# The turn from attention to the MLP: last residual rows in temporary tiles, later stores, block pieces at other steps, one weight load issued earlier

## The chip, the core and the metric

The kernel runs on one core of a Trainium2 chip. A core has TensorE (matrix products, into PSUM), VectorE (DVE), ScalarE (ACT), GpSimd (POOL) and SyncE (SP), each working through its own instructions in order. SyncE's queue issues nearly all transfers between the chip's memory and the core's SBUF; 16 DMA engines carry them out. The metric is the device time of one execution in microseconds (us); lower is better.

## The reference

One layer of an encoder over x of 2048 tokens x 1024 features, all in float32:

```python
sh1, sc1, gt1, sh2, sc2, gt2 = split(silu(c) @ w_ada + b_ada, 6)
h = rmsnorm(x, g_norm1) * (1 + sc1) + sh1
q_sb, k_sb, v_sb, q_ca, k_ca, v_ca = split(h @ w_in)
o_sb = stick_breaking_attention(q_sb, k_sb, v_sb)      # 8 heads of 64, strictly causal
o_ca = chunked_relpos_attention(rmsnorm(q_ca, g_q), rmsnorm(k_ca, g_k), v_ca, rel_bias)
                                                       # 8 heads, own chunk of 64 + 8 before
x = x + gt1 * (concat(o_sb, o_ca) @ w_o)               # the output projection
h = rmsnorm(x, g_norm2) * (1 + sc2) + sh2
x = x + gt2 * (square(relu(h @ w1)) @ w2)              # the MLP, 1024 -> 4096 -> 1024
```

## The kernel before

Everything is held transposed: 128 features in the partitions, tokens along the free axis, in four token blocks `g` of 512 (`TB`), handled in the order 3, 2, 1, 0. A tile of 128 x 512 float32 is 256 KB. To keep float32 accuracy each operand is split into a high part (`act.copy` into float32r) and a low part (DVE: source minus high), and each product is three matmuls (`mm3`: high x high, high x low, low x high).

**Attention with filler.** After the input projections the attention units run in a loop of steps. Into its steps are woven single matmuls of a "filler": first input projections still missing, then the output projection `outproj(g)` of finished token blocks. A filler is a generator: it yields 1.0 after each matmul, and at the end of a row a function that finishes the row. One row `n` of `outproj` is 128 output features: 8 x 3 matmuls of the weights `ow` (1 MB, from `scr_wo`, ring of three buffers) with the attention output `fx`. At the start of row `n` the weights of row `n + 2` and the residual input `xr` of row `n + 1` are loaded. `finish_row` calls `residual`: DVE adds the gated row to `xr`, and the store of `xr` to `scr_x` is appended to the list `stores`.

**The turn.** When the attention loop ends, rows 3 to 7 of block 1 and all of block 0's output projection are left. `drain.append(True)` marks it, attention's pools are closed, and the MLP's pools are opened over the same memory (`temp`: 7 tiles, `kept`: 12 tiles, `opp`: 8 operand tiles). Then a hand-written list runs. `row()` finishes the matmuls of the current row and its residual, sends stores down to one left over, and starts the next row (its loads, its first matmul). Between the rows stand `steps[0].fetch(a, b)`, which loads operand tiles `opm` a to b - 1 of block 0's output projection (0.5 MB each from `scr_m`), and `some(k, m)`, piece `m` of operand block `k`.

**Operand blocks.** The MLP works on two halves of the tokens, first blocks 3 and 2 (`mb` = 1), with a seven-product scheme (Strassen's) for each 2 x 2 arrangement of tiles. `right_blocks(1, k)` for k = 0 to 3 makes the seven right operands `h` (`hops[i, k]`) of product `i` out of four stored rows. Its pieces are: 0, `load`: four loads of 256 KB from `scr_x` (`ty` for block 0, `cy` for the others); 1, `scale`: four multiplications on DVE, four affine steps and three high parts on ACT; 2, `mixed`: five DVE operations, two high parts on ACT; 3, `rest`: six DVE operations, two high parts on ACT.

**The Mixed and First steps.** After the last row a list `steps` runs, one entry at a time. The first eight are `Mixed` (the output projection of block 0, rows 5, 6, 7, 0, 1, 2, 3, 4; rows 5 to 7 find their weights still in the ring). Mixed step `n` is 24 matmuls (`pso`) over `opm` 0 to 7 and then a residual (`cxr`); `then()` loads the weights `wo` of the step three on, and from step 5 the first weights of the MLP (`w`, two loads of 512 KB), and has POOL form four sums of them (`ts`). Then come `First` steps, 12 matmuls each (4 blocks `k` x 3), in the order of products 1, 6, 5, 7, 2, 3, 4. Work can be tied to a step with `at(n, job)`: it is placed ahead of the step's matmuls. The left operands of the first two First steps, `opr`, are split at a place written by hand:

```python
            if n == KT - 2:
                firsts = spare.tile([P, 2, 2, TB], F32R, tag="r8", name="opr")
                for m in range(2):
                    steps[KT + m].prepare(firsts[:, m])
```

**Order on the queues.** In the turn SyncE keeps program order too (`osp`). Each transfer signals one of eight completion semaphores, taken in turn over all transfers of SyncE and ScalarE; a transfer is issued only when the eighth before it has landed, and when the tile it writes is free. A matmul on TensorE, DVE's and ACT's operations keep the order of the program.

Of the kernel before, what the change touches and what calls it, by code (L numbers as in the profile page):

```python
# [9 lines left out]
F32 = mybir.dt.float32  # L10
# [8 lines left out]
P = 128  # L19
# [5 lines left out]
KT = D // P  # L25
TB = 512
# [53 lines left out]
def encoder_kernel(ctx, tc, xT, c, g1, g2, w_in, w_rest, gqk, bias, w_o, w1, w2, w_ada, b_ada, out):  # L80
# [142 lines left out]
        )  # L223


    stores = []

    def residual(g, n, ps, xr):
        dve.scalar_tensor_tensor(xr, ps, mod[:, 2 * KT + n : 2 * KT + n + 1], xr, op0=ALU.mult, op1=ALU.add)
        stores.append(lambda: sp.dma_start(scr_x[g, n], xr))  # L230

    def load_residual(g, n, pl):
        xr = pl.tile([P, TB], F32, tag="xr", name=f"xr{g}_{n}")
        sp.dma_start(xr, xT[n * P : (n + 1) * P, g * TB : (g + 1) * TB])
        return xr

# [6 lines left out]
    if True:  # L243
# [260 lines left out]
        first = (2, 0, 1)  # L504
# [151 lines left out]
    if True:  # L656
# [317 lines left out]
        def outproj(self, g):  # L974
            yield lambda k: scr_m[g, k]

            def load(n):
                w = ring.tile([P, 2, KT, P], F32R, tag="r8", name=f"ow{g}_{n}")
                sp.dma_start(w.bitcast(F32), scr_wo[n,])
                return w  # L980

            mx = self.moving()
            ws = [load(0), load(1)]
            rx = load_residual(g, 0, xrp)
            yield "wait"
            for n in range(KT):
                w, xr = ws.pop(0), rx
                if g == 1:
                    resident[n] = w
                if n + 2 < KT:  # L990
                    ws.append(load(n + 2))
                if n + 1 < KT:
                    rx = load_residual(g, n + 1, xrp)
                else:
                    yield "ahead"
                ps = dense.tile([P, TB], F32, tag="ps", name=f"po{g}_{n}")
                for k in range(KT):
                    for i, (l, m) in enumerate(((0, 0), (0, 1), (1, 0))):
                        pe.matmul(
                            ps, w[:, l, k, :], mx[k][:, m, :], start=k == 0 and i == 0, stop=k == KT - 1 and i == 2  # L1000
                        )
                        yield 1.0
                yield lambda n=n, ps=ps, xr=xr: finish_row(g, n, ps, xr)
# [46 lines left out]
        weight = STEPS * sum(u.weight for u in units) + LAG * 0.6  # L1050
        credit = 0.0
        rest = 0
        late, soon, first, drain = [], [], [], []

        def fill(part):

# [20 lines left out]
        def force(f):  # L1077

            got = next(f.gen, None)
            if callable(got):  # L1080
                got()
            return None if got is None else callable(got)
# [87 lines left out]
    if True:  # L1170
# [25 lines left out]
        def temp(nm):  # L1196
            return tp.tile([P, TB], F32, tag="t", name=f"t{nm}")
# [9 lines left out]
        def at(n, job):  # L1207
            jobs.setdefault(n, []).append(job)
# [343 lines left out]
        for mb in (1, 0):  # L1552
            begin = len(steps)
            steps += [First(mb, j, i) for j in range(NP) for i in PRODUCTS]
            for j in range(NP):
                f = steps[begin + 7 * j]
# [22 lines left out]
        def some(k, *ns):  # L1579
            for n in ns:  # L1580
                blocks[k][n]()
# [3 lines left out]
        def row():  # L1585

            while force(left) is False:
                pass
            while len(stores) > 1:
                stores.pop(0)()  # L1590
            return force(left)

        steps[0].fetch(0, KT // 2)
        row()
        steps[0].fetch(KT // 2, KT - 2)
        some(0, 0)
        row()
        some(0, 1)
        steps[0].fetch(KT - 2, KT)
        row()  # L1600
        some(0, 2)
        some(1, 0)
        row()
        some(0, 3)
        some(1, 1)
        while row() is not None:
            pass
        while stores:
# [4 lines left out]
            del resident[n]  # L1613
        for m in range(LEFT):
            steps[m].load()
        at(0, lambda: some(2, 0))
        at(3, lambda: some(3, 0))
        for n, (k, m) in enumerate(((1, 2), (1, 3), (2, 1), (2, 2), (2, 3), (3, 1), (3, 2), (3, 3))):
            at(n, lambda k=k, m=m: some(k, m))
        ready, used = KT, 0  # L1620
        ahead = iter(steps[1:])
        nxt = next(ahead)
        for n, s in enumerate(steps):
            while nxt is not None and ready - used + nxt.tiles <= 8:
                nxt.prepare()
                ready += nxt.tiles
                nxt = next(ahead, None)
            for m in (0, 1) if n == 0 else (n + 1,):
                if m < KT:
                    steps[m].load_row()  # L1630
            if n == KT - 2:
                firsts = spare.tile([P, 2, 2, TB], F32R, tag="r8", name="opr")
                for m in range(2):
                    steps[KT + m].prepare(firsts[:, m])
            for job in jobs.get(n, ()):
                job()
            s.run()
            used += s.frees
            later.tick()
# [41 lines left out]
```

## Time and profile before

| | |
|---|---|
| median of 3 runs | 2691.01 us |
| lowest and highest | 2685.60 and 2695.53 us |
| the profiled execution | 2683.0 us |
| its span, first to last instruction | 2681.1 us |
| mean granted TensorE clock | 0.992 |
| TensorE busy | 2600.1 us, 97% |
| HBM read and written | 457.21 and 191.37 MB, 242 GB/s over the span |

The span is the time from the first to the last instruction of the profiled execution; the run's own time is 1.9 us longer. All times inside the trace count from the start of the span. "Busy" counts an engine's instructions, not its waiting; an idle stretch carries in brackets what ended it. "SPq" and "ACTq" are instructions that issue transfers. A program line of L42 is a helper that records the operation, so the tile names tell which part of the kernel a row belongs to.

### The profile page before, as it was taken

The numbers are of one execution on the slowest core, as the hardware profiler recorded it, in microseconds if no ns is written. First come the engines' busy times: TensorE is split into PE (matmuls) and PEld (weight loads), VectorE is DVE, ScalarE is ACT, GpSimd is POOL, SyncE is SP. The second block draws the span as 40 slices with busy tenths as digits, with TensorE's granted clock in tenths as the row PEclk, the third lists the DMA queues.
The fourth block names the chain that finished last, engine by engine and source line by source line (L and its number), as shares of the span: only waits on it lengthen the run. The fifth ranks groups of instructions, "written<-read, shape, count | busy, mean of one in ns | idle before, by whom it ended". The sixth has DMA issues, their size and how long they took to land. (4 is left out here: it accounts for less than half of the span.)

```text
span 2681.1 us, 40293 instructions
## 1 busy us (share of the span) xinstructions
PE 2600.1 (97%) x12944; PEld 2162.3 (81%) x12944; DVE 1919.8 (72%) x3287; ACT 1510.9 (56%) x2962; POOL 921.3 (34%) x1192
## 2 busy tenths in 40 slices
PE   7999999898999999999999999999999999999999
PEld 5888887687878887788877888878888888888887
DVE  7656766697789878889756777767857566655565
ACT  5333436786788778778644444456544445444443
POOL 4330145575566656777512233200002323200000
PEclk9999999999999999999999999999999999999999
DMA  9879888978887687756666777686675343465574
GB/s 340 306 300 364 308 322 256 265 255 275 252 255 247 203 269 246 232 190 211 211 231 248 278 256 273 252 334 219 217 265 188 138 165 138 149 243 194 198 267 157
DMA packets 263061, 651.28 MB, mean 243 GB/s; under 512 B 29632, under 2 KB 61376, under 8 KB 252992
## 3 DMA queue, kind: packets, MB, share of 16 engines
q1 hardware_dynamic: 261552, 643.98, 70.4%
q10 hardware_dynamic: 1296, 4.72, 0.4%
q8 instruction: 103, 1.69, 0.3%
q14 instruction: 110, 0.90, 0.1%
HBM read 457.21 MB, written 191.37 MB: 242 GB/s over the span
## 5 line engine op out<-in xcount | busy, mean ns | idle before, releaser
L42 PE MATMUL ps<-oph,opv 128*128 128x512 f32 x2688 | 612.0, 389 | 0.2
L42 PE MATMUL ps<-h,opw 128*128 128x512 f32 x2664 | 608.6, 391 | 1.9 <-DVE cx L42 1.9
L42 PEld LDWEIGHTS ps<-oph,opv 128*128 128x128 f32 x2688 | 504.0, 188 | 106.3 <-DVE opv L42 1.2
L42 PEld LDWEIGHTS ps<-h,opw 128*128 128x128 f32 x2664 | 502.6, 189 | 107.8 <-DVE cx L42 2.6
L42 POOL TENSOR_TENSOR b<-b,p 128x512 f32<-128x512 f32 (+1 forms) x320 | 359.6, 1124 | 196.4 <-DVE p L42 176.1
L42 DVE TENSOR_TENSOR wtl<-wt,wth 128x512 fp32r<-128x512 f32 (+3 forms) x544 | 290.0, 544 | 50.5 <-ACT wth L42 48.1
L42 ACT CAST wth<-wt 128x512 fp32r<-128x512 f32 (+3 forms) x544 | 257.5, 484 | 116.1 <-PE wt L42 101.2
L42 DVE TENSOR_TENSOR oph<-hw,oph 128x512 fp32r<-128x512 f32 x224 | 155.1, 692 | 222.0 <-ACT oph L42 222.0
L42 ACT CAST oph<-hw 128x512 fp32r<-128x512 f32 x224 | 139.3, 622 | 283.7 <-PE ps L42 267.1
L42 PE MATMUL pt<-w,ht 128*128 128x512 f32 x1248 | 289.0, 391 | 2.9 <-DVE qh L42 2.2
L42 POOL TENSOR_TENSOR ts<-w 128x512 f32<-128x512 f32 x32 | 46.8, 1462 | 680.1 <-DMA w<-in_w_dram 332.2
L42 PEld LDWEIGHTS pt<-w,ht 128*128 128x128 f32 x1248 | 232.8, 188 | 51.6 <-ACT csq L42 2.9
L42 DVE TENSOR_TENSOR_SCAN p<-z,p,zero 128x512 f32<-128x512 f32 x192 | 246.0, 1281 | 33.6 <-ACT z L42 28.2
L42 PE MATMUL acc<-wth,v 128*128 128x512 f32 (+3 forms) x544 | 221.9, 412 | 2.1 <-ACT otmp L42 2.1
L42 ACT ACTIVATE b<-z 128x512 f32<-128x512 f32 (+1 forms) x320 | 171.6, 536 | 64.8 <-PE z L42 46.8
L42 PE MATMUL z<-k,q 128*128 128x512 f32 (+3 forms) x640 | 186.1, 373 | 9.8 <-DVE p L42 7.1
L42 POOL TENSOR_TENSOR e<-e,cols 128x640 f32<-128x640 f32 (+4 forms) x128 | 142.9, 1121 | 147.2 <-DVE cols L42 89.9
L42 PE MATMUL acc<-wtl,v 128*128 128x512 f32 (+3 forms) x544 | 186.4, 349 | 0.0
L42 PE MATMUL wt<-ident,b 128*128 128x128 f32 x1088 | 172.5, 274 | 6.7 <-DVE cols L42 5.1
L42 DVE TENSOR_TENSOR opw<-w,opw 128x512 fp32r<-128x512 f32 x127 | 96.8, 764 | 113.2 <-ACT opw L42 113.1
L42 PE MATMUL po<-fx,ow 128*128 128x512 f32 x576 | 166.4, 404 | 6.0 <-DMA ow<-scr_wo 6.0
L42 ACT ACTIVATE z<-z 128x512 f32<-128x512 f32 (+1 forms) x320 | 170.7, 533 | 0.0
(192 smaller groups left out, 4222.0 us busy)
## 6 DMA issues: line engine op xcount, KB each, us to landing
hw<-scr_hid SPq DMA_DIRECT2D x112, 512.0 KB, 3.9
k<-scr_k SPq DMA_DIRECT2D x272, 128.0 KB, 4.1
v<-scr_v SPq DMA_DIRECT2D x136, 256.0 KB, 4.2
q<-scr_q SPq DMA_DIRECT2D x128, 256.0 KB, 5.2
w<-in_w_dram SPq DMA_DIRECT2D x64, 512.0 KB, 5.2
hw<-scr_s SPq DMA_DIRECT2D x64, 512.0 KB, 4.6
fw<-scr_w SPq DMA_DIRECT2D x28, 1024.0 KB, 6.8
wa<-in_w_ada_dram SPq DMA_DIRECT2D x48, 512.0 KB, 6.7
```

Of the source, the lines that this page charges most:

```text
L42: return lambda *x, **y: self.tc.keep_in_program_order(f(*x, **y))
```

## The change

1. `drain` is made at the same place as `stores`, so that `load_residual` can ask for it. Once attention is over, the residual inputs of rows 5, 6 and 7 go to `temp` tiles; before, they took the three `xrp` tiles in turn, each of which is free when the row three before has been stored.
2. `row()` leaves up to two stores pending, not one.
3. The hand-written list: two rows follow each other before the first piece of block 0, so that starting the second one issues row 7's weights (`ow` 7) ahead of the four block loads and of `opm` 4 and 5. Pieces (0, 3) and (1, 1) move from the rows into the first Mixed step.
4. The remaining pieces of blocks 1 to 3 are placed in Mixed steps 0 to 6, two in each of the first five; before, they took steps 0 to 7.
5. The split of `opr` moves from ahead of Mixed step 6 to ahead of Mixed step 7.

```diff
-    stores = []
+    stores, drain = [], []
...
     def load_residual(g, n, pl):
-        xr = pl.tile([P, TB], F32, tag="xr", name=f"xr{g}_{n}")
+        xr = temp(f"xr{g}_{n}") if drain else pl.tile([P, TB], F32, tag="xr", name=f"xr{g}_{n}")
...
-        late, soon, first, drain = [], [], [], []
+        late, soon, first = [], [], []
...
-            while len(stores) > 1:
+            while len(stores) > 2:
                 stores.pop(0)()
             return force(left)
 
         steps[0].fetch(0, KT // 2)
         row()
+        row()
+        some(0, 0)
         steps[0].fetch(KT // 2, KT - 2)
-        some(0, 0)
         row()
         some(0, 1)
         steps[0].fetch(KT - 2, KT)
         row()
         some(0, 2)
         some(1, 0)
-        row()
-        some(0, 3)
-        some(1, 1)
         while row() is not None:
             pass
...
-        at(0, lambda: some(2, 0))
-        at(3, lambda: some(3, 0))
-        for n, (k, m) in enumerate(((1, 2), (1, 3), (2, 1), (2, 2), (2, 3), (3, 1), (3, 2), (3, 3))):
-            at(n, lambda k=k, m=m: some(k, m))
+        pieces = ((0, 3), (1, 1)), ((1, 2), (2, 0)), ((1, 3), (2, 1)), ((2, 2), (3, 0)), ((2, 3), (3, 1)), ((3, 2),), ((3, 3),)
+        for n, now in enumerate(pieces):
+            for k, m in now:
+                at(n, lambda k=k, m=m: some(k, m))
...
-            if n == KT - 2:
+            if n == KT - 1:
                 firsts = spare.tile([P, 2, 2, TB], F32R, tag="r8", name="opr")
                 for m in range(2):
                     steps[KT + m].prepare(firsts[:, m])
```

## The prediction

> **What bounds the kernel now.** I read the page first, then the list of who TensorE waited for, then TensorE's timeline where it waited.
>
> ```profile
> span 2681.1 us, 40293 instructions
> PE 2600.1 (97%) x12944; PEld 2162.3 (81%) x12944; DVE 1919.8 (72%) x3287; ACT 1510.9 (56%) x2962; POOL 921.3 (34%) x1192
> ```
>
> TensorE is the bound: only time in which it idles or runs slowly can be won. From 1460 us to the end it waits once, and that place is not touched:
>
> ```profile
> PE ps L42 <- DVE cx L42: 1.9, 1, 1.9
> ```
>
> The turn from attention to the MLP lies at 1367 to 1460 us. Its TensorE timeline (start, length, in brackets the idle time before and its releaser; `po` are the last rows of token block 1, `pso` the eight Mixed steps, `opr` the first two First steps):
>
> ```profile
> 1366.91 16.58 PE L42 MATMUL po<-fx,ow 128*128 128x512 f32 x72
> 1389.47 8.24 PE L42 MATMUL po<-fx,ow 128*128 128x512 f32 x24 [5.98 <-DMA ow<-scr_wo]
> 1397.55 16.48 PE L42 MATMUL pso<-opm,ow 128*128 128x512 f32 x72
> 1413.87 27.36 PE L42 MATMUL pso<-opm,wo 128*128 128x512 f32 x120
> 1441.07 2.43 PE L42 MATMUL ps<-h,opr 128*128 128x512 f32 x10
> 1444.62 2.79 PE L42 MATMUL ps<-h,opr 128*128 128x512 f32 x11 [1.12 <-DVE h L42]
> 1449.54 0.79 PE L42 MATMUL ps<-h,opr 128*128 128x512 f32 x1 [2.13 <-ACT h L42]
> 1450.69 1.22 PE L42 MATMUL ps<-h,opr 128*128 128x512 f32 x2 [0.36 <-DVE h L42]
> 1451.71 10.67 PE L42 MATMUL ps<-h,opw 128*128 128x512 f32 x36
> ```
>
> The pace is (1441.07 - 1413.87)/120 = 0.2267 us a matmul, so a row or a Mixed step of 24 takes 5.44 and a First step of 12 takes 2.72. Two stalls:
>
> - First stall. Rows 4 to 6 could end at 1366.91 + 72 x 0.2267 = 1383.23; row 7 starts at 1389.47, 6.24 late, and takes 8.08 instead of 5.44, 2.64 more. Together 8.88.
> - Second stall. The 24 `opr` matmuls take 1451.71 - 1441.07 = 10.64 instead of 5.44: 5.20. The next 36 take 10.51 (10.67 less the 0.16 by which a last matmul outlasts the pace) instead of 8.16: 2.35. Together 7.55.
>
> So at most 8.88 + 7.55 = 16.4 us are there, 0.6% of the run. The granted clock says what the slow parts are (stretch, its length, busy time by engine, then clock, DMA share, GB/s):
>
> ```profile
> 1366.90:1383.50 16.60, 16.59 (x75) 13.39 (x73) 2.89 (x4) 1.95 (x3) 1.29 (x1) 1.00 0.84 291
> ...
> 1389.50:1397.50 8.00, 8.00 (x24) 6.38 (x25) 6.41 (x11) 2.48 (x4) 0.00 (x0) 0.66 0.72 238
> ...
> 1452.00:1460.30 8.30, 8.30 (x28) 6.17 (x28) 8.30 (x8) 4.06 (x8) 6.63 (x4) 0.74 0.95 334
> ...
> 1411.50:1424.10 12.60, 12.60 (x58) 10.42 (x57) 10.87 (x18) 6.97 (x11) 0.00 (x0) 1.00 1.03 382
> ...
> 1750.00:1780.00 30.00, 28.14 (x120) 22.53 (x118) 21.75 (x37) 19.76 (x36) 1.81 (x5) 0.94 0.99 371
> ```
>
> After each stall the clock is low (0.66, 0.74), and so it is, at 0.94 over 30 us, after the single 1.9 us wait above.
>
> **Why the first stall is there.** SyncE's queue, then its waits, then the transfers of the turn with their time to landing:
>
> ```profile
> 1366.34 0.32 SPq L42 DMA_DIRECT2D ow<-scr_wo  x1
> 1366.99 0.33 SPq L42 DMA_DIRECT2D xr<-in_xT_dram  x1
> 1367.38 10.84 SPq L42 DMA_DIRECT2D opm<-scr_m  x2
> 1378.26 1.85 SPq L42 DMA_DIRECT2D ty<-scr_x  x4
> ...
> 1380.69 0.38 SPq L42 DMA_DIRECT2D ow<-scr_wo  x1
> ```
>
> ```profile
> SPq L42 <- DVE cxr L42: 17.4, 3, 14.0
> ...
> SPq L42 <- DMA scr_x<-xr: 11.0, 2, 5.8
> SPq L42 <- DMA scr_m<-os: 10.1, 1, 10.1
> ```
>
> ```profile
> DMA packets 7567, 22.11 MB, mean 307 GB/s; under 512 B 836, under 2 KB 836, under 8 KB 6668
> ...
> wo<-scr_wo SPq DMA_DIRECT2D x5, 1024.0 KB, 7.2
> ...
> ow<-scr_wo SPq DMA_DIRECT2D x2, 1024.0 KB, 8.0
> ...
> w<-in_w_dram SPq DMA_DIRECT2D x2, 512.0 KB, 7.1
> ...
> scr_m<-os SPq DMA_DIRECT2D x1, 512.0 KB, 2.9
> scr_m<-os ACTq DMA_DIRECT2D x1, 512.0 KB, 7.4
> ```
>
> The program uses eight completion semaphores in turn, so a DMA starts only when the eighth DMA before it has landed. Between the two `opm` loads the queue stands 10.1 us, because the second is the eighth after attention's last store (`scr_m<-os`, on ScalarE's queue). Behind it wait four block loads, a store and, at 1380.69, row 7's weights.
>
> **Part 1: weights first.** Two rows now stand ahead of the block loads and of `opm` 4 and 5. Row 7's weights wait only for their ring buffer, which row 4 frees at 1366.91 + 5.44 = 1372.35, and, as eighth, for attention's last store but one on SyncE, landed 2.9 us after its issue, before all this. They land at 1372.4 + 8.0 = 1380.4, 2.8 before row 7 wants them at 1383.23. What moves behind them, `opm` 4 to 7 (2 MB), is wanted from 1388.67 + 4 x 0.68 = 1391.4 on. Between them stands xr6, now the eighth after the ACT store, so it starts where that `opm` started, at about 1378; the block loads follow at 1378.4 instead of 1378.26, `opm` 4 at 1380.3. At 291 GB/s the 3.75 MB from xr6 to `opm` 7 (xr6 0.25, block 1, two `opm` 1, store 3 and xr7 0.5, two `opm` 1) take 12.9 us from 1378 on: 1391 for `opm` 7, wanted at 1393.4. TensorE does not stop: 8.88 won, Mixed starts at 1388.67, First at 1441.07 - 8.88 = 1432.19.
>
> **Part 2: temporary tiles, late stores.** The residual loads of rows 5 to 7 no longer wait for the stores of rows 2 to 4; two such waits were 11.0 us of SyncE. By itself this is worth nothing, since row 7's weights are now ahead. Seven temporaries exist: 3 rows and the 4 of block 0 fill them. The first sums of the MLP reuse those of row 5, row 6 and block 0's first; by then (1428, below) rows 5 and 6, done by 1383.23, are long stored. A later store costs nothing: its reader stands 104 MLP steps on.
>
> **Part 3: blocks and `opr`.** The second stall is DVE's and ACT's order:
>
> ```profile
> 1382.03 0.69 DVE L42 TENSOR_TENSOR ty<-ty,r 128x512 f32<-128x512 f32 x1 [8.63 <-DMA ty<-scr_x]
> ...
> 1394.53 1.46 DVE L42 TENSOR_TENSOR h<-ty,h 128x512 fp32r<-128x512 f32 x2
> ...
> 1411.58 2.49 DVE L42 TENSOR_TENSOR cy<-cy,r 128x512 f32<-128x512 f32 x4
> ...
> 1422.58 1.46 DVE L42 TENSOR_TENSOR h<-cy,h 128x512 fp32r<-128x512 f32 x2
> ...
> 1441.76 1.11 DVE L42 TENSOR_TENSOR opr<-ts,opr 128x512 fp32r<-128x512 f32 x1 [3.35 <-ACT opr L42]
> 1442.80 2.36 DVE L42 TENSOR_TENSOR h<-cy,h 128x512 fp32r<-128x512 f32 x2
> ```
>
> ```profile
> 1437.07 0.62 ACT L42 CAST opr<-w 128x512 fp32r<-128x512 f32 x1 [6.25 <-DMA w<-in_w_dram]
> 1441.11 0.62 ACT L42 CAST opr<-ts 128x512 fp32r<-128x512 f32 x1 [3.42 <-POOL ts L42]
> ```
>
> The split `opr` is put ahead of block 3's last two pieces and waits for the MLP's first weights; block 3 starts only at 1442.80, and TensorE waits for its `h`; SyncE waits 14.0 us behind the same DVE. Now block 3 comes first (steps 5 and 6) and `opr` last (step 7). No instruction is added: each block stays 15 DVE operations. Is DVE in time? Block 0 starts with its loads, as before, and ended at 1394.53 + 1.46 = 1396.0. Block 2, from 1411.58 to 1424.04, is the price of one block with two residuals: 12.46, some 0.6 of it waiting for TensorE. Three more end between 1396.0 + 3 x 11.8 = 1431.4 and 1396.0 + 3 x 12.46 = 1433.4, and `opr`'s first low half 0.7 later, 1432.1 to 1434.1. First's third matmul wants it at 1432.19 + 0.45 = 1432.64. That is the tight place: from nothing to 1.5 us are lost; I take 0.5, near the middle. The second `opr`: weights issued at the end of step 5, 1432.19 - 2 x 5.44 = 1421.3, land at 1428.4 to 1429; two POOL sums and one cast (in the profile 1441.73 - 1437.07 = 4.7 from the first load's landing) give 1433.1 to 1433.7, DVE's 1.11 1434.2 to 1434.8; wanted at 1432.19 + 2.72 + 0.45 = 1435.4. In time. The next weights also start earlier, against TensorE, than before.
>
> What a stall of 1 to 2 us costs beside itself: by the row 1750 to 1780, 0.06 x 30 = 1.8 us of clock, by none at the least. The Trainium skill's page "TensorE: Matmul & The Clock Gate", Part 1, says the clock is halved after an idle window of about 3.4 us; by that rule a short stall costs only itself. The rows disagree: no single wait of the second stall is over 2.13, yet the clock was 0.74 after it.
>
> **Sum.** 8.88 + 7.55 - 0.5 = 15.9. The profiled execution took 2683.0 (span 2681.1 and 1.9 around it), so 2667.1 of it; the median of the runs is 2691.0, 8.0 more, which nothing here changes: **2675** for a median. I call 0.5% (13.5 us) what a measurement of this kernel can tell from no change.
>
> **Rivals.**
>
> - Transfers, priced on the shared engines. The early 1 MB flows beside attention's last store, on which xr6 waits, and ahead of xr6 and the block loads. It takes 3.6 us at 291 GB/s; where all of it comes on top, block 0 and with it `opr` come 3.6 later, and with 1.8 of clock the gain is 15.9 - 5.4 = 10.5: 2680.5, no change. For it: DMA share 0.84 in that stretch. Against: an `opm` of half the size leaves that place. The Trainium skill's page "DMA: Bandwidth & Descriptors", section "Issuing engines are not separate DMA queues", says that transfers of all issuing engines run on the same 16 engines and interleave, which is this mechanism.
> - One half does not work: xr5's tile, taken from attention's memory, is late and holds the weights behind it (gain 7.5), or `opr` stays late (gain 8.9): 2682 to 2683.5. Against: attention's last readers there are TensorE's, done by 1366.91.
> - Slower: the Mixed steps become bound by transfers. 22.11 MB in 72 us would have to flow in 63, 351 GB/s instead of 307. If 307 is the limit, the 8.88 come back as a wait in each step, each followed by a slow clock of 2.64: with five steps -16.4 + 8.9 + 13.2 = +5.7, 2697; only with all eight, +13.6, does it pass 0.5%. For it: weights land after 7.2 (median) of the 10.9 they have. Against: 382 GB/s from 1411.5 to 1424.1.
>
> **Numbers.** Forecast 0.60, transfers 0.22, one half 0.11, slower 0.07, of which 0.04 beyond 0.5%. So faster 0.60, same 0.36, slower 0.04. Low end: all 16.4, the 1.8 of clock in 1750 to 1780 gone too, and the 5.4 by which the fastest run lies under the median: 2667. High end: one half alone, 2683.5, and the 4.5 by which the slowest run lies over it: 2688.
>
> **What would show it.** Right: row 7 follows row 6 without idle, its clock is 1.00; the `ow` issue stands near 1372.5; First starts near 1432; DVE's block 3 stands before `opr`; no wait for `h`. Wrong: a TensorE wait for `opm`, `wo` or `opr` in the Mixed or First steps, or `ow` still issued near 1380.

## The result, and the profile after

| | before | changed |
|---|---|---|
| median | 2688.01 us | 2668.46 us |
| lowest and highest | 2685.15 to 2695.53 us | 2666.92 to 2673.90 us |
| profiled execution, its span | 2683.0, 2681.1 us | 2673.9, 2672.1 us |

The ratio is 0.9929, interval 0.9909 to 0.9949: 13.7 to 24.5 us faster. Beside it on two other chips the changed kernel had 0.9951 (0.9938 to 0.9963) and 0.9950 (0.9936 to 0.9963), which is 13.7 and 12.8 us. The forecast was 16 faster, and a median of 2675; the median came out 6.5 lower, and 3.0 of that is before's own median (2688.01 with five runs, 2691.01 with the three that the forecast had). By the 0.5% that the prediction calls the least a measurement can tell, the first ratio (0.71%) is clear and the two repeats (0.49% and 0.50%) stand at the edge. The ratios are of means; differences in us are of medians, so the two need not agree to the last us.

The page of the changed kernel, the two lines that stand in the prediction for before:

```profile
span 2672.1 us, 40291 instructions
...
PE 2598.4 (97%) x12944; PEld 2162.5 (81%) x12944; DVE 1929.1 (72%) x3287; ACT 1511.7 (57%) x2962; POOL 919.8 (34%) x1192
```

TensorE's timeline of the turn in the changed kernel (the columns as before; a row is one run of matmuls without a pause):

```profile
1369.96 22.02 PE L42 MATMUL po<-fx,ow 128*128 128x512 f32 x96
1391.82 16.48 PE L42 MATMUL pso<-opm,ow 128*128 128x512 f32 x72
1408.14 27.36 PE L42 MATMUL pso<-opm,wo 128*128 128x512 f32 x120
1435.34 5.60 PE L42 MATMUL ps<-h,opr 128*128 128x512 f32 x24
1440.78 297.55 PE L42 MATMUL ps<-h,opw 128*128 128x512 f32 x1308
1742.63 4.61 PE L42 MATMUL ps<-h,opw 128*128 128x512 f32 x12 [4.30 <-DVE cx L42]
```

Both stalls are gone: the rows `po` are one run of 96, the Mixed steps follow, the 24 `opr` matmuls take 5.6 and 1308 matmuls follow them without a pause. The granted clock agrees (changed kernel: rows, Mixed steps, first First steps; stretch, length, busy time by engine, then clock, DMA share, GB/s):

```profile
1369.90:1391.80 21.90, 21.90 (x99) 18.13 (x98) 9.00 (x14) 6.32 (x10) 1.29 (x1) 1.00 0.99 366
1391.80:1435.30 43.50, 43.50 (x193) 36.04 (x192) 37.61 (x61) 23.43 (x37) 2.38 (x2) 1.00 0.95 342
1435.30:1461.00 25.70, 25.70 (x115) 21.26 (x114) 20.93 (x22) 12.38 (x22) 15.30 (x11) 1.00 0.50 189
```

**A measure for the turn.** The single profiles differ by several us ahead of the turn (row 4 starts between 1364.31 and 1372.47 in the thirteen), so I measure from the start of row 4 to the end of the First steps that ends in the wait for `cx`. For the changed kernel that is 1742.63 - 4.30 - 1369.96 = 368.4; for before, with the row below, 1752.73 - 1.85 - 1366.91 = 384.0. The turn is 15.6 us shorter. The 384.0 stands alone: before has one profile, the one from which the prediction read its stalls.

```profile
1752.73 4.61 PE L42 MATMUL ps<-h,opw 128*128 128x512 f32 x12 [1.85 <-DVE cx L42]
```

The two profiled spans differ by only 9.0, since this profile reached the turn 3.05 later (1369.96 against 1366.91; nothing before it was changed, and the two repeats reached it at 1368.36 and 1372.47), and its wait for `cx` was 4.30 instead of 1.85. -15.6 + 3.05 + 2.45 is -10.1; the other 1.1 lies behind.

SyncE's queue in the changed kernel, which answers to the one of before:

```profile
1375.69 0.32 SPq L42 DMA_DIRECT2D ow<-scr_wo  x1
1379.05 0.33 SPq L42 DMA_DIRECT2D txr<-in_xT_dram  x1
1379.44 2.49 SPq L42 DMA_DIRECT2D ty<-scr_x  x4
1381.98 0.97 SPq L42 DMA_DIRECT2D opm<-scr_m  x2
```

Row 7's weights are issued 5.73 after the start of row 4, 3.4 ahead of the residual input that waits for attention's last store; before, they were issued 13.8 after it, behind all the others.

### The profile page after: what moved, and what is told of

Same layout as the page of the kernel before. It is cut to its first block, busy times and chain, and to the rows that moved or that the text cites. A ratio compares the mean times of both kernels' runs of the same rounds, so it can differ in the third digit from the quotient of the medians.

```text
span 2672.1 us, 40291 instructions
## 1 busy us (share of the span) xinstructions
PE 2598.4 (97%) x12944; PEld 2162.5 (81%) x12944; DVE 1929.1 (72%) x3287; ACT 1511.7 (57%) x2962; POOL 919.8 (34%) x1192
## 5 line engine op out<-in xcount | busy, mean ns | idle before, releaser
L42 DVE TENSOR_TENSOR opw<-w,opw 128x512 fp32r<-128x512 f32 x127 | 103.8, 819 | 113.1 <-ACT opw L42 113.0
L42 PEld LDWEIGHTS wt<-ident,b 128*128 128x128 f32 x1088 | 134.8, 142 | 37.9 <-DVE cols L42 6.7
```

The lines of the kernel that those rows point to most:

```text
L42: return lambda *x, **y: self.tc.keep_in_program_order(f(*x, **y))
```

## The experiments

Each run is told by its time against before on the same chip and by the length of its turn, measured as above (before 384.0, changed 368.4). Single runs of one kernel on one chip lie up to 14 us apart (before beside the repeat: 2680.41 to 2694.59), while the changed kernel's turn is 368.4, 368.2 and 367.5 in its three profiles; so where the two disagree by 1 to 3 us the turn is the finer of the two.

**The changed kernel again.** No edit; it is the measure for the others on two chips.

> The changed kernel once more, to stand beside the others on the same chip. In the traces the stretch from the first matmul of rows 4 to 7 to the last First step is 15.6 us shorter than before; so 14 to 17 us faster than before, and no wait of TensorE between row 4 and the end of the First steps but the one on cx.

> The changed kernel as it is, as the measure for the other two on this chip. Own theory: the turn from row 4 to the end of the First steps takes 368 us as in the two profiles before, 15 to 16 less than before the change, and the time is 13 to 20 us under before.

Measured: 13.7 and 12.8 us faster; turns of 368.2 and 367.5. They are 0.3 and 0.2 short of the times expected of them; the turns are as expected, and TensorE waits nowhere between row 4 and the wait for `cx`.

**Part 3 alone** (before, with the new places of the pieces and of `opr`):

```diff
-        at(0, lambda: some(2, 0))
-        at(3, lambda: some(3, 0))
-        for n, (k, m) in enumerate(((1, 2), (1, 3), (2, 1), ...
+        pieces = ((1, 2), (2, 0)), ((1, 3), (2, 1)), ((2, 2), (3, 0)), ((2, 3), (3, 1)), ((3, 2),), ((3, 3),)
...
-            if n == KT - 2:
+            if n == KT - 1:
```

> The kernel before with opr at step 7 and the pieces of blocks 1 to 3 in steps 0 to 5, one step earlier than in e4_blocks_only; rows, tiles, stores as before. Own theory (in e4 block 3 came late because step 0 held no piece and DVE waited 4.8 us for the step's residual, and its last six operations then met POOL's sums, which stretched them from 0.68 to 1.75): block 3 is done before the sums begin, the second stall goes, the first stays: 6 to 9 us faster than before. Rival (without the new rows the blocks cannot come in time, whatever their steps): waits for h or opr of 3 us or more stay, 2 to 5 faster as in e4.

Measured: 0.9969 (0.9957 to 0.9980), 7.2 us faster; turn 376.2, 7.8 shorter. Its TensorE timeline:

```profile
1390.64 8.57 PE L42 MATMUL po<-fx,ow 128*128 128x512 f32 x24 [4.87 <-DMA ow<-scr_wo]
...
1415.98 27.48 PE L42 MATMUL pso<-opm,wo 128*128 128x512 f32 x120 [0.45 <-DMA wo<-scr_wo]
1443.30 5.60 PE L42 MATMUL ps<-h,opr 128*128 128x512 f32 x24
1448.74 51.62 PE L42 MATMUL ps<-h,opw 128*128 128x512 f32 x227
```

The first stall stands; of the second nothing is left. So part 3 alone removes the second stall, at a price close to the forecast 7.55.

**Parts 1 and 2 alone** (the changed kernel with `opr` at `KT - 2` and the old places of the pieces of blocks 1 to 3, except that (0, 3) and (1, 1) stay in Mixed step 0):

> The changed kernel with the old places of the block pieces of blocks 1 to 3 and the old place of opr: parts 1 and 2 alone. Own theory, two stalls that add up: row 7 follows row 6 without a wait, so the 8.9 us of the first stall are won, and the second stall is there at its old size, 7.6: 7 to 9 us faster than before. Rival, the second stall grows: DVE's blocks are bound by DVE's own work and do not start earlier, so a First that starts 8.9 us earlier waits for them that much longer: under 4 us faster, with a wait for h or opr over 8 us in all. From the run with opr early (7.3 us of the turn lost) I lean to something between, 5 to 7.

Measured: 0.9974 (0.9962 to 0.9985), 7.2 us faster; turn 1744.54 - 3.10 - 1364.32 = 377.1, 6.9 shorter. Its TensorE timeline:

```profile
1386.18 16.48 PE L42 MATMUL pso<-opm,ow 128*128 128x512 f32 x72
...
1429.70 2.43 PE L42 MATMUL ps<-h,opr 128*128 128x512 f32 x10
1433.51 2.83 PE L42 MATMUL ps<-h,opr 128*128 128x512 f32 x11 [1.38 <-DVE h L42]
1438.43 0.51 PE L42 MATMUL ps<-h,opr 128*128 128x512 f32 x1 [2.09 <-ACT h L42]
1439.58 0.98 PE L42 MATMUL ps<-h,opr 128*128 128x512 f32 x2 [0.65 <-DVE h L42]
1440.37 1.05 PE L42 MATMUL ps<-h,opw 128*128 128x512 f32 x2
...
1744.54 5.49 PE L42 MATMUL ps<-h,opw 128*128 128x512 f32 x12 [3.10 <-DVE cx L42]
```

Rows 4 to 7 are one run of 96 matmuls from 1364.32 on, up to the Mixed steps. The second stall is back, although First starts 65.4 after row 4 (1429.70 - 1364.32) and not 74.2 as before (1441.07 - 1366.91), 8.8 earlier: the `opr` matmuls take 1440.37 - 1429.70 = 10.67, against 10.64 before. A wait of 1.74 for `cx` at 1454.86, which before does not have, comes on top, and from the start of First to the wait at the end the run takes 1.9 longer than before. So the second stall grows little, and not by the 8.8 that the first one gives: the rival expected with this run falls, and my leaning to 5 to 7 was just too low. The weights of `opr` are issued 10.7 before First starts in both (1419.02 here, 1430.38 before), so they, and DVE's block behind them, move with TensorE. The two halves, 7.2 us each by time (6.9 and 7.8 by turn), come to 14.4 (14.7), against 13.7 and 12.8 for the whole on these two chips (15.6 by turn): within chance they add, as the forecast had it.

**`opr` early** (the changed kernel, one place):

```diff
-            if n == KT - 1:
+            if n == KT - 2:
```

> The changed kernel with one line undone: the split of opr stands ahead of Mixed step 6 again. Own theory (the second stall is opr standing ahead of block 3's pieces): now only piece (3, 3) stands behind opr, six DVE operations of 0.6 us; the sixth product's operand of block 3 is then ready about when TensorE wants it, so 0 to 2 us are lost, with up to 1.8 of slow clock: 14 to 19 us faster than before. Rival (the moved split alone removed the second stall): 7.5 us come back, 9 to 12 faster than before.

Measured: 0.9973 (0.9963 to 0.9984), 6.3 us faster only; turn 375.7, 7.3 longer than the changed kernel. My expectation missed, and so did the rival's 9 to 12 faster; what came back in the turn, 7.3, is near the rival's 7.5. DVE, then TensorE, of this run:

```profile
1427.62 0.69 DVE L42 TENSOR_TENSOR opr<-w,opr 128x512 fp32r<-128x512 f32 x1 [3.89 <-ACT opr L42]
1431.69 1.11 DVE L42 TENSOR_TENSOR opr<-ts,opr 128x512 fp32r<-128x512 f32 x1 [3.39 <-ACT opr L42]
```

```profile
1436.97 0.73 PE L42 MATMUL ps<-h,opr 128*128 128x512 f32 x2 [0.58 <-DVE h L42]
...
1439.66 5.28 PE L42 MATMUL ps<-h,opw 128*128 128x512 f32 x22 [1.38 <-DVE opw L42]
1448.60 11.64 PE L42 MATMUL ps<-h,opw 128*128 128x512 f32 x43 [3.66 <-ACT cu L42]
```

DVE stands idle 3.89 + 3.39 = 7.28 us for `opr`, with one piece of block 3 and two residuals queued behind. I had counted only the late `h`; that is 0.58. What I had not followed is the queue behind it: the residuals are late, so SyncE holds their stores, and behind the stores the next weights:

```profile
1423.75 14.95 SPq L42 DMA_DIRECT2D scr_x<-cxr  x2
1438.80 0.88 SPq L42 DMA_DIRECT2D w<-in_w_dram  x2
```

ACT stands 3.36 for these weights and 3.38 for POOL's sums of them, and the copy `cu`, for which TensorE waits, stands behind that on ACT. TensorE pays 3.66 for it a step later, and the clock is 0.61 over the next 4.4 us. In the changed kernel the place of this one split is worth about as much as the whole second stall.

**Part 3 in another form** (before, as in "part 3 alone", but with nothing in Mixed step 0 and every set one step later):

```diff
+        pieces = (), ((1, 2), (2, 0)), ((1, 3), (2, 1)), ((2, 2), (3, 0)), ((2, 3), (3, 1)), ((3, 2),), ((3, 3),)
```

> The kernel before with only the new places of the pieces in the Mixed steps (blocks 1 to 3 by step 6) and of opr (step 7); rows, tiles, stores as before. Own theory: the first stall stays (wait of 6 us for ow, 8.9 with the clock), the second goes (no wait for h): 7 to 9 us faster than before. Rival (the second stall is a follower of the first, the blocks being late because the rows were): waits for h stay, 0 to 3 faster.

Measured: 0.9983 (0.9973 to 0.9993), 3.1 us faster; turn 381.6, only 2.4 shorter. Missed; the rival's 0 to 3 is near, but not its waits for `h`: TensorE waits for `opr`. TensorE of this run, its DVE, and POOL beside it:

```profile
1443.14 1.22 PE L42 MATMUL ps<-h,opr 128*128 128x512 f32 x2 [3.70 <-ACT opr L42]
```

```profile
1407.65 0.75 DVE L42 SCALAR_TENSOR_TENSOR cxr<-pso,mod,cxr 128x512 f32<-128x512 f32 x1 [4.82 <-DMA cxr<-in_xT_dram]
...
1434.05 0.68 DVE L42 TENSOR_TENSOR cy<-cy,cy 128x512 f32<-128x512 f32 x1
...
1436.78 1.77 DVE L42 TENSOR_TENSOR cy<-cy,cy 128x512 f32<-128x512 f32 x1
```

```profile
1435.02 1.29 POOL L42 TENSOR_TENSOR ts<-w 128x512 f32<-128x512 f32 x1 [64.06 <-DMA w<-in_w_dram]
...
1437.97 1.73 POOL L42 TENSOR_TENSOR w<-w 128x512 f32<-128x512 f32 x1
```

Two costs in place of the stall. With no piece in step 0, DVE has nothing to do before the first Mixed residual and stands 4.82 for it. And block 3, late by that, runs beside POOL's sums of the weights, where four operations take 1.55 to 1.77 each instead of 0.68. The split of `opr` comes behind all this on ACT and DVE. So it is not enough to put `opr` last. In the run with the sets one step earlier (above), which differs in this alone and wins 7.2, block 3 ends at 1437.86, just before POOL begins at 1437.93; that the overlap with POOL is the greater part of the difference is argued, since no run moved POOL's sums.

**The weights behind the blocks** (the changed kernel with the old order of row 7's weights):

```diff
         row()
-        row()
-        some(0, 0)
         steps[0].fetch(KT // 2, KT - 2)
+        some(0, 0)
+        row()
         row()
```

> The changed kernel with the old order of row 7's weights: behind opm 4 and 5 and the four block loads; temporary tiles, late stores, block pieces and opr stay new. Own theory (row 7's weights are late because the queue waits for attention's last store): a wait of about 6 us for ow before row 7 comes back, with a slow clock behind it, 8.9 together, so 7 to 11 us faster than before. Rival (the waits for stores made the weights late, and temporary tiles removed them): no wait, 16 to 19 faster.

Measured: 0.9961 (0.9949 to 0.9973), 10.3 us faster; turn 373.5, 5.1 longer than the changed kernel. SyncE's queue and TensorE of this run:

```profile
1367.07 10.77 SPq L42 DMA_DIRECT2D opm<-scr_m  x2
...
1379.85 0.37 SPq L42 DMA_DIRECT2D ow<-scr_wo  x1
```

```profile
1387.18 7.31 PE L42 MATMUL po<-fx,ow 128*128 128x512 f32 x24 [4.00 <-DMA ow<-scr_wo]
```

The queue stands between the two `opm` loads as it did before, and row 7 waits: the mechanism of the first stall is the forecast one. It is smaller than in the profile of before (4.26 late and 1.71 of slow row, 6.0, instead of 8.9). The stall is not a fixed price: with part 3 alone it is 1390.64 - 1385.51 = 5.1 and 3.0, 8.1, and in part 3's other form 6.6. Attention's last store is not what differs: it lands 7.3 to 7.4 after its issue in all four profiles with the old order. What differs is how long row 7's weights take to land (8.6 before, 7.2 to 7.6 in the others) and the slow row behind them (2.64 before, 1.5 to 3.0 in the others).

**The old tiles** (the changed kernel without part 2), tried on two chips:

```diff
-        xr = temp(f"xr{g}_{n}") if drain else pl.tile([P, TB], F32, tag="xr", name=f"xr{g}_{n}")
+        xr = pl.tile([P, TB], F32, tag="xr", name=f"xr{g}_{n}")
...
-            while len(stores) > 2:
+            while len(stores) > 1:
```

> The changed kernel with residual tiles and store rule as before (three tiles in turn, one store left over); order of the rows, pieces and opr stay new. Own theory (prediction, part 2: worth nothing by itself): xr6 waits for store 3, issued just ahead of row 7's weights, about as long as for attention's last store; xr7 waits for store 4 and holds opm 6 and 7 back by some 4 us, about their slack: 0 to 2 us slower than the changed kernel, 16 to 19 faster than before. Rival (the waits for stores were the first stall): 8.9 come back, 9 to 11 faster than before.

> The changed kernel with the residual rows in the old three tiles and one store pending, beside the changed kernel on the same chip. If temporary tiles and late stores are worth something, TensorE waits again 1 to 2 us in all for opm 6 and 7 and the time is 1 to 3 us over the changed kernel. If they are worth nothing, as was predicted, no wait for opm is seen and the times lie within 1 us of each other.

Measured: 0.9959 (0.9944 to 0.9973), and on the other chip 0.9955 (0.9942 to 0.9967), where the changed kernel beside it had 0.9950: 0.8 us between the medians, with intervals that overlap. The first run is 13.8 faster than before and not the 16 to 19 expected; of the second expectation both sides hold in part, the wait and the time within 1 us. TensorE of the second run, and its queue:

```profile
1392.27 0.98 PE L42 MATMUL pso<-opm,ow 128*128 128x512 f32 x3 [0.98 <-DMA opm<-scr_m]
1393.91 11.85 PE L42 MATMUL pso<-opm,ow 128*128 128x512 f32 x51 [0.67 <-DMA opm<-scr_m]
```

```profile
1386.95 0.33 SPq L42 DMA_DIRECT2D xr<-in_xT_dram  x1
1387.34 0.90 SPq L42 DMA_DIRECT2D opm<-scr_m  x2
```

Row 7's weights still come early without part 2, but by less: a store now stands ahead of them, which makes them the eighth after attention's last store, so SyncE stands 6.6 for it and issues them 9.3 after row 4's start (5.7 in the changed kernel). They land 4.8 later, 2.2 before row 7 wants them. And the residual input of row 7 waits 5.8 for a store, and `opm` 6 and 7 stand behind it: 1.65 us of waits on TensorE here, 1.44 on the other chip. First starts 67.6 and 67.4 after row 4, 2.2 and 2.0 later than in all three profiles of the changed kernel (65.4); the turns are 371.7 and 370.2, 3.3 and 1.8 longer. So part 2 is worth about 2 us in the traces; in the time a difference is not shown.

**An extra megabyte** (the changed kernel with a load of 1 MB that nobody reads, ahead of the block loads):

```diff
+        extra = spare.tile([P, 2, KT, P], F32R, tag="r8", name="extra")
+        sp.dma_start(extra.bitcast(F32), scr_wo[0,])
```

> The changed kernel with one useless load of 1 MB (weights into a free tile) put between row 7's weights and the four block loads. Own theory (the transfers have slack: row 7's weights land 3.5 us early, the first half of opr is ready 2.9 early, the second 1.2): blocks come some 3 us later, 0 to 3 us slower than the changed kernel, a short wait for opr or opm at most. Rival (the turn is bound by its transfers): the load's 3.6 us come back in full with 1.8 of slow clock, 5 or more slower than the changed kernel.

Measured: 0.9951 (0.9938 to 0.9965), 2668.16 us against 2670.36 of the changed kernel beside it: no loss. The turn is 369.5, 1.3 longer than in the profile beside it (368.2). What the engines show (the same 24 us in the changed kernel on the same chip and in this run; row 4 starts at 1368.36 in the one and 1364.62 in the other):

```profile
1366.00:1390.00 24.00, 24.00 (x114) 20.03 (x113) 9.74 (x16) 6.80 (x12) 1.29 (x1) 1.00 1.00 359
```

```profile
1366.00:1390.00 24.00, 24.00 (x107) 19.85 (x107) 9.50 (x16) 6.35 (x10) 1.29 (x1) 1.00 1.00 380
...
1431.44 5.29 PE L42 MATMUL ps<-h,opr 128*128 128x512 f32 x22 [0.83 <-DVE opr L42]
```

At 359 GB/s, 1 MB is 2.9 us. The rate rose to 380 (counted over the 24 us from row 4's start, from 365 to 377), and DVE's block 0 came 17.3 after the start of row 4 instead of 15.7, 1.6 later. In the profile beside it `opr` was ready 1.2 before it was wanted; here it came 0.9 late, with block 3's last two operations stretched from 1.46 to 2.38 beside POOL, and cost TensorE 0.83. So the rival of the transfers has its mechanism, but even a second megabyte costs it about 1 us.

**Second's first load earlier** (the changed kernel, and another place): the wait for `cx` that follows the turn in all these profiles.

```diff
-                at(n - 7, steps[n].load)
+                at(n - (7 if n > begin + 7 * NP else 10), steps[n].load)
```

> The changed kernel with one more edit: the first load of the Second steps is issued ten steps ahead instead of seven. Theory: the wait for cx at the end of the First steps (1.9 us before, 4.3 after) comes from ACT standing 7 us on that load, with DVE behind it; with the load 8 us earlier the wait and the half-clock windows after it (3.4 to 6.8 us) go: 3 to 7 us faster than the changed kernel, 18 to 23 faster than before. Rival (DVE is simply full there): the wait stays, no change.

Measured: 2664.85 us, 0.9928 (0.9916 to 0.9941) of before, 5.5 less than the changed kernel beside it (2670.36). This version is faster than both. TensorE's only wait from row 4 to 1760 us in this run, a short one behind the place where the first profile of the changed kernel waited 4.30 and the one beside this run 3.40, and its clock there:

```profile
1744.04 8.80 PE L42 MATMUL ps<-oph,opv 128*128 128x512 f32 x36 [0.42 <-ACT opv L42]
```

```profile
1726.00:1744.00 18.00, 17.62 (x78) 14.27 (x76) 11.65 (x19) 9.40 (x17) 0.00 (x0) 1.00 1.02 368
```

The wait for `cx` is gone and the clock stays at 1.00. From row 4's start to the end of the span it is 1295.4, against 1302.1, 1300.8 and 1299.2 in the three profiles of the changed kernel. In the changed kernel ACT had stood 7.00 for the operand `hw` of the first Second step, DVE behind ACT, and the sum `cx`, which TensorE needed, behind DVE.

## Why the prediction was right, point by point

- **The first stall, 8.88.** It went whole. The issue stands 5.73 after row 4's start (forecast 5.6) and lands 7.1 later, 3.5 before row 7 wants the weights (forecast 2.8). The run with the old order brought the wait back through the same queue. As a size, 8.88 was that one profile's: 6.0, 6.6 and 8.1 in the three others with this stall. One working in this part is slightly off and changes nothing: 3.75 MB of 1024 KB each take 13.5 us at 291 GB/s, not 12.9, so `opm` 7 was due at 1391.5, still before 1393.4.
- **The second stall, 7.55.** It went whole, and alone it is worth 7.2 us by time and 7.8 by turn. That the split's place decides was right, and stronger than I said: `opr` early costs 7.3 us of turn even with the blocks early. That it need only stand last was too simple: in part 3's other form it did, and TensorE waited 3.70 for it.
- **The tight place, 0.5 lost.** Nothing was lost. DVE in the changed kernel:

```profile
1396.52 2.49 DVE L42 TENSOR_TENSOR cy<-cy,r 128x512 f32<-128x512 f32 x4
...
1419.92 2.49 DVE L42 TENSOR_TENSOR cy<-cy,r 128x512 f32<-128x512 f32 x4
...
1430.20 1.46 DVE L42 TENSOR_TENSOR h<-cy,h 128x512 fp32r<-128x512 f32 x2
...
1432.24 0.68 DVE L42 TENSOR_TENSOR opr<-w,opr 128x512 fp32r<-128x512 f32 x1
1436.18 1.11 DVE L42 TENSOR_TENSOR opr<-ts,opr 128x512 fp32r<-128x512 f32 x1 [3.26 <-ACT opr L42]
```

  Two blocks take 23.4 (1419.92 - 1396.52), one 11.7, just under my range of 11.8 to 12.46, and `opr`'s low half ends at 1432.92, 2.9 before First's third matmul at 1435.34 + 0.45; in the two repeats it is 1.2 and 2.5. Block 0 ended 26.6 after row 4's start (1396.52 - 1369.96), and not 29.1 as I had held it (1396.0 - 1366.91): the residual input that waits for attention's last store was issued 9.1 after that start (1379.05), and I had taken 11.1. That store lands 5.5 after its issue here and 4.5 to 5.6 in all nine profiles with the weights first, against the 7.3 to 7.4 with the old order; half a megabyte (`opm` 4) no longer flows beside it, which may be why. That is the term that was mis-sized, 0.5 for 0; the place is tight, as the 1.2 and the extra megabyte show.
- **Part 2, "by itself worth nothing".** This step was wrong, by about 2 us in the traces: without it TensorE waits 1.4 to 1.65 us for `opm` 6 and 7. My step left out that `opm` 6 and 7 stand behind the residual input of row 7, and that the one store which part 2 holds back would have put row 7's weights behind attention's last store. In the time the difference (0.8 us) is not shown. The sum is not touched, since part 2 was in place.
- **The sum, 15.9.** The turn gives 15.6. The medians give 19.5 (13.7 to 24.5), and 13.7 and 12.8 in the repeats; 15.9 lies among them. That the turn comes within 0.3 is in part luck and in part built in: the 16.4 was read from the same profile of before as the 384.0, in which the first stall was larger than in the three others. What the experiments show is that both stalls go, each by its own half of the change, and 12.8 to 19.5 us with them. The profiled pair shows 9.0, for the reasons above, none of which is shown to be the change's.
- **The rivals.** Transfers: a second megabyte cost 1.3 us of turn, not the 5.4 it was priced at, while the engines moved 359 to 380 GB/s where I had 291; and attention's last store, which the early megabyte was to hold up, landed sooner than before. One half alone: each half was run, 7.2 us each, and both work in the changed kernel. Slower: no Mixed step waited. I had asked for 351 GB/s and feared a limit of 307; over the Mixed steps it was 342, over the rows 366, about 350 over both.
- **Left open.** The wait for `cx` was 1.85 in the one profile of before that is shown and 2.7 to 4.4 in all the others, except where the load was put earlier. Whether that is chance of one profile is not shown.

## What to carry to other kernels

Two stalls at one seam added up here, each with its own cause, and the trace of before could price them within 1 to 3 us: late start plus slow clock, from the timeline. For every instruction that waits for a transfer, follow what stands behind it on its engine and on the queue that waits for that engine; here a split at the wrong place cost more through the loads held behind it than through the operands it delayed. After a seam is closed, look at the next one: the wait at the end of the First steps was worth 5.5 us for one number.

## What the hardware showed that was not expected

- **DVE beside POOL.** An operation with two inputs took 0.68 alone and 1.77 beside POOL's sums, whose own went from 1.29 to 1.73 (rows under "Part 3 in another form"). The Trainium skill's page "SBUF — State Buffer", section "SBUF: two separate sides", says that such a DVE operation and a GpSimd operation lock the same port pair for a whole instruction; the rows agree in kind: each engine's operation then takes about 1.75, not its own 0.68 or 1.29.
- **The clock after a short wait.** The matmuls behind the wait for `cx`, in the changed kernel (after a wait of 4.30), in before (after 1.85), and in the changed kernel on the third chip (after 2.92):

```profile
1742.60:1747.00 4.40, 4.37 (x12) 3.47 (x13) 1.96 (x3) 3.68 (x7) 0.00 (x0) 0.61 0.97 291
```

```profile
1752.70:1757.00 4.30, 4.27 (x12) 3.37 (x13) 1.99 (x4) 4.08 (x8) 0.00 (x0) 0.60 0.92 305
```

```profile
1742.80:1747.20 4.40, 4.35 (x19) 3.62 (x20) 1.98 (x3) 3.89 (x7) 0.00 (x0) 1.00 0.95 304
```

  A wait of 1.85 was followed by a clock of 0.60, a longer one of 2.92 by 1.00. The Trainium skill's page "TensorE: Matmul & The Clock Gate", Part 1, has the clock halved after an idle window of about 3.4 us; 1.85 is under that, so the length alone does not decide here.
